# A decoder layer on one core: the first loads in another order and on a second queue, early transposes moved, and the sample-state products grouped in other blocks

## The chip, the core and the metric

One NeuronCore of one Trainium2 chip runs the whole program. The metric is device microseconds (us) of one launch, the median of several runs. Engines: TensorE (PE in the profile; its weight loads are PEld), VectorE (DVE), ScalarE (ACT), GpSimd (POOL) and SyncE (SP, which here only issues DMAs). "q" behind an engine's name means its instruction queue, where DMAs are issued.

## The reference

One inference step of one layer (`DEPTH` is 1) for 256 prompt tokens and 8 x 4 sample tokens, all in fp32, model width 2048:

```python
proj = x @ w_in
gB, gC, h, q, k, v, z, b_logit, a_logit, m_a, m_b = jnp.split(proj, split_points, axis=-1)
conv_out, new_conv_a = causal_depthwise_conv(gC * h, conv_a_buf, conv_a_w)
y_a = (gB * conv_out) @ w_a_out
qkv, new_gdn_buf = causal_depthwise_conv(jnp.concatenate([q, k, v], -1), gdn_buf, gdn_conv_w)
...
o, S = gated_delta_rule(qh, kh, vh, g, beta, S0.astype(jnp.float32))
o = o * lax.rsqrt(jnp.mean(o * o, -1, keepdims=True) + NORM_EPS) * gdn_norm_w
o = o * jax.nn.silu(z)
y_b = o @ w_b_out
merged = jax.nn.sigmoid(m_a) * y_a + jax.nn.sigmoid(m_b) * y_b
x = layer_norm(ALPHA * x + merged @ w_o, ln1_g, ln1_b)
hid = jnp.square(jax.nn.relu(x @ w_up))
x = layer_norm(ALPHA * x + hid @ w_down, ln2_g, ln2_b)
```

It returns the two outputs and the new convolution and delta-rule states. The delta rule keeps a 128 x 128 state S for each of 8 heads of each sample; the new sample states are an output of 4 MB.

## The kernel before, in words

**Tokens as columns.** All 288 tokens (256 prompt, 32 sample) are the moving columns of TensorE's products; 128 x 128 pieces of the weights are the stationary operand. x arrives token by row, so TensorE turns it (transposes against `ident`, L965 for prompt, L949 for samples) into tiles of 128 features by 288 tokens. Every fp32 factor is split into a high and a low part (`xh`, `xl`; `hi`, `lo`), and each product is done as three: `xh*hi` and `xl*hi` (L216), `xh*lo` (L218).

**Blocks.** The weights are cut into blocks of 512 KB (`blocks`), and the main loop (L1672) goes through them one by one. A block passes four steps: `load(i)` brings `raw` by a DMA issued on SyncE's queue (L174); `split_hi` casts it to `hi` on ScalarE (L184); `split_lo` subtracts on VectorE, `lo = raw - hi` (L139), and with that frees the `raw` buffer; `matmuls(i)` does its 24 products. `raw`, `hi` and `lo` have four buffers each. In the steady part, loop step i casts and subtracts for block i + 3 (`AHEAD`) at its beginning and issues the load of block i + 7 at its end. That load has to wait for `split_lo` of block i + 3, which frees the buffer. Every engine works its instructions in the order in which the loop emits them.

**The first block.** Block 0 is two groups of columns for half the depth: for `k` = 0, 1 and for each of the two `members` (`u`), six products: two `xh*hi`, two `xl*hi`, two `xh*lo`. Its raw weights come in parts: `w_first(0, 0, 1)` and `w_first(0, 1, 2)` are the halves for k = 0 (128 KB each), `w_first(1)` the 256 KB for k = 1. x comes in parts as well: `x_first(a, b)` brings columns a to b of the first 512 features. `fill` is a list of closures; `matmuls` pops one behind each `xh*lo` product. `second_tile` (two turns, the copies of x for k = 1, and the casts of the weights for k = 1) and `second_half` (the turns for the next block's two tiles) are put there. `warm_up(n, u)` issues n products of zeros on `128 * u` columns, which nothing reads.

**The sample states.** The generator `gdn(G)` does the delta rule of head group G, and its inner generator `sample` (L1447) the samples' part; both run one step per block, between the casts and the block's products. At its end `sample` goes over four heads `hh`: `spread(hh)` makes `vm[hh]` by eight ScalarE multiplications (L1496); for `j` = 0, 1 a product of 512 columns (`pn`, L1508) goes to one of four PSUM buffers (`gtile`), and four VectorE instructions add it to `S0[:, hh]` (L142, `S<-S,gexp,g`) and with that free the buffer; `store(hh - 1)` sends 512 KB of new states out on GpSimd's queue (L1517). `spread(hh + 1)` is emitted at the beginning of head `hh`. A `yield` before a product moves it to the next block; for G = 1 two of the eight products have none and stand in one block with the product before them.

**Around it, at blocks 106 to 112** (392 to 415 us in the trace): the same blocks carry, in `gdn(1)`, the output norm: squares on ScalarE (L1574, L1575), a scaling (`sq`, L1578), a square root with its table load (L1580), then on VectorE `so`, the reciprocal (L1581), a scaling of the output `xt` (L139) and its transpose (L1585). The loop emits `split_lo` behind them. Block 111 also holds the evacuation of z's third group (`sz`, L384, with a table load for Silu), which stands on ScalarE behind the cast for block 114; it frees the PSUM buffer `acc` into which block 112 (the first of the merge gates) begins to write.

Of the kernel before, what the change touches and what calls it, by code (L numbers as in the profile page):

```python
# [16 lines left out]
P = 128  # L17
# [13 lines left out]
C_GB, C_GC, C_H, C_Q, C_K, C_V, C_Z, C_BA, C_MA, C_MB = (  # L31
    0, 1024, 2048, 3072, 4096, 5120, 6144, 7168, 7184, 9232)

GW = 256
# [67 lines left out]
def hybrid_kernel(ctx: ExitStack, tc: tile.TileContext, A):  # L102
# [16 lines left out]
    def nm(s):  # L119
        counter[0] += 1  # L120
        return f"{s}{counter[0]}"
# [13 lines left out]
    act, dve, pe, gps, sp = nc.scalar, nc.vector, nc.tensor, nc.gpsimd, nc.sync  # L135
# [11 lines left out]
    w_in = A["w_in"][0]  # L147
# [8 lines left out]
    raw, his, los = {}, {}, {}  # L156
    due = {}
    fill = []
# [5 lines left out]
    def load(i, steps=(), between=()):  # L164
        if i >= len(blocks):
            return
        gi, r0, k0, _, _ = blocks[i]
        t = wp.tile([P, KB, GW], F32, tag="raw", name=nm("raw"))
        kb, cols = gi["kb"], gi["cols"]
        dst = t.rearrange("p k c -> p (k c)").rearrange("p (k c) -> p k c", k=kb)  # L170
        src = gi["W"][r0:r0 + kb * P, gi["col0"]:gi["col0"] + cols].rearrange("(k p) c -> p k c", p=P)
        k = 0
        for step in steps or (kb,):
            sp.dma_start(dst[:, k:k + step], src[:, k:k + step])  # L174
            k += step
            if between:
                between.pop(0)()
        raw[i] = t
# [14 lines left out]
    def matmuls(i):  # L193
        gi, r0, k0, first, last = blocks[i]
        if gi.get("by_token"):
            return first_tokens(i, k0)
        members = gi.get("pair", (gi,))
        if first:
            for m in members:
                m["ps"] = acp.tile([P, 2, 512], F32, tag="acc", name=nm("acc"))  # L200
        ps = members[0]["ps"]
        h, l = his.pop(i), los.pop(i)
        ah, al = gi["acts"]()
        n = gi["width"]
        kb = gi["kb"]
        h, l = (u.rearrange("p k c -> p (k c)").rearrange("p (k c) -> p k c", k=kb) for u in (h, l))
        for k in range(kb):
            xh_, xl_ = ah[:, k0 + k, 0:n], al[:, k0 + k, 0:n]
            st = first and k == 0
            en = last and k == kb - 1  # L210
            per = gi["cols"] // P // len(members)
            for u, m in enumerate(members):
                ts = [(m["ps"][:, t, 0:n], slice((per * u + t) * P, (per * u + t + 1) * P)) for t in range(per)]
                both = [(o, c, x) for o, c in ts for x in (xh_, xl_)]
                for o, c, x in both[::2] + both[1::2] if i == 0 else both:
                    pe.matmul(o, h[:, k, c], x, start=st and x is xh_, stop=False)  # L216
                for o, c in ts:
                    pe.matmul(o, l[:, k, c], xh_, start=False, stop=en)  # L218
                    if fill:
                        fill.pop(0)()  # L220
        if last:
            for n, f in enumerate(gi["evac"]):
                at(i + 1 + n, lambda f=f: f(ps))
# [666 lines left out]
    def warm_up(n, u=4):  # L890
        for _ in range(n):
            pe.matmul(wps.rearrange("p (u c) -> p u c", u=4)[:, 0:u], warm, bmid(warm, u), start=True, stop=True)
# [14 lines left out]
    def x_first(a, b):  # L907
        sp.dma_start(xr[0][:, :, a:b], xpr[:, :, a:b])
# [1 line left out]
    def x_sample_in(c, queue=sp):  # L910
        queue.dma_start(xs4[:, c * P:c * P + P], xsr[c])

    def w_first(k, a=0, b=2):
        sp.dma_start(raw[0][:, 2 * k + a:2 * k + b, :],
                     w_in[k * P:k * P + P, C_K + GW * a:C_K + GW * b].rearrange("p (u c) -> p u c", c=GW))

    x_first(0, 128)
    x_sample_in(0, act)
    w_first(0, 0, 1)
    w_first(0, 1, 2)  # L920
    x_first(128, 512)
    w_first(1)
    load(1)
    sp.dma_start(xr[1], xpr[:, :, 512:1024])
    x_sample_in(1)
# [21 lines left out]
    def x_sample(i):  # L947
        g = gtile()
        pe.transpose(g[:, 0:P], xs4[:, i * P:(i + 1) * P], ident)  # L949
        gv = g[:, 0:P].rearrange("p (t j) -> p j t", j=4)  # L950
        xv, xw = (u[:, 4 * i:4 * i + 4, NP_:NT] for u in (xh, xl))

        def out(copy=act.copy):
            copy(xv, gv)  # L954
            tt(xw, gv, xv, SUB)
        return out
# [188 lines left out]
    def gdn(G):  # L1145
# [214 lines left out]
        both = Tm.rearrange("p q (j k) -> p q j k", j=8)  # L1360
# [86 lines left out]
        def sample():  # L1447

            sp1 = gtile()
            pe.matmul(sp1[:, 0:128], kst, kst, start=True, stop=True)  # L1450
            pe.matmul(sp1[:, 128:256], kst, qst, start=True, stop=True)
            pe.transpose(sp1[:, 384:512], vfs.rearrange("p h b t -> p (h b t)"), ident)
            stt(Es, G_["s_row"][:, G], G_["s_ngc"][:, G:G + 1], cst("mbias4"), ADD, ADD)
            act.activation(Es, Es, AF.Exp)
            act.mul(vs, sp1[:, 384:512], snk)
            act.mul(kr, kr, sc[:, 0:1])
            stt(nMs, sp1[:, 0:128], sc[:, 2:3], Es, MUL, MUL)
            stt(aTs, sp1[:, 128:256], srk, Es, MUL, MUL)
            n4, u4, t4, r4 = (Ts[:, 4 * u:4 * u + (16 if u == 3 else 4)] for u in range(4))
            dve.tensor_reduce(out=n4, in_=nMs.rearrange("p (b j) -> p j b", j=4), axis=mybir.AxisListType.X, op=ADD)  # L1460
            tt(n4, n4, cst("i4u"), MUL)
            tt(n4, n4, cst("i4"), ADD)
            sp.dma_start(four_d[G].rearrange("b k j -> (b k) j"), n4)
            yield
            sp.dma_start(r4, four_d[G].rearrange("b k j -> b (k j)").unsqueeze(1).to_broadcast([32, 4, 16]))
            yield from quarters(kr3, kr, 0)
            if G:
                yield
            rows4 = r4.rearrange("p (k j) -> p k j", k=4)
            dve.tensor_copy(u4, cst("i4"))  # L1470
            for j in range(1, 4):
                tt(t4[:, 0:j + 1], u4[:, 0:j + 1], rows4[:, 0:j + 1, j], MUL)
                dve.tensor_reduce(out=u4[:, j:j + 1], in_=t4[:, 0:j + 1], axis=mybir.AxisListType.X, op=ADD)
            tt(Us.rearrange("p (b j) -> p b j", j=4), u4.unsqueeze(1).to_broadcast([P, 32, 4]),
               cst("l4").rearrange("p (b j) -> p b j", j=4), MUL)
            stt(vs, kso[:, 0, :], G_["s_neg"][:, G:G + 1], vs, MUL, ADD)
            act.mul(osm, kso[:, 1, :], G_["s_eg"][:, G:G + 1])
            yield
            pv_ = gtile()
            pe.matmul(pv_[:, 0:P], Us, vs, start=True, stop=True)  # L1480
            act.mul(vns, pv_[:, 0:P], sc[:, 1:2])
            v3 = pl.tile([P, 4, P], F32R, tag="U", name=nm("v3"))
            yield from quarters(v3, vns, 1)
            yield
            po = gtile()
            pe.matmul(po[:, 0:P], aTs, vns, start=True, stop=True)
            tt(osm, osm, po[:, 0:P], ADD)
            done.append(1)
            vm = {}


            def spread(hh):
                if hh < 4:
                    vm[hh] = pl.tile([P, 8, P], F32R, tag=("vmh", "vml")[hh % 2], name=nm("vm"))
                    for b in range(8):
                        act.mul(vm[hh][:, b], v3[:, hh].bitcast(F32), cst("bmask")[:, b:b + 1])  # L1496

            spread(0)
            yield
            for hh in range(4):  # L1500
                spread(hh + 1)
                if hh:
                    store(hh - 1)
                for j in range(2):
                    if G == 0 or (hh, j) not in ((2, 0), (3, 1)):
                        yield
                    pn = gtile()
                    pe.matmul(pn, kr3[:, hh], vm[hh][:, 4 * j:4 * j + 4, :], start=True, stop=True)  # L1508
                    for u in range(4):
                        b = 4 * j + u  # L1510
                        stt(S0[:, hh, b], S0[:, hh, b], G_["egls"][:, b, 4 * G + hh:4 * G + hh + 1],
                            pn[:, u * P:u * P + P], MUL, ADD)
            yield
            store(3)
# [9 lines left out]
        o = T([P, 4, 2, P], "xt")  # L1524
# [123 lines left out]
    idle = lambda: None  # L1648
    turns(t0[0:2])
    xs_out = x_sample(0)  # L1650
    warm_up(1, 2)
    act.copy(h0[:, 0], t[:, 0])
    o0[0](dve.tensor_copy)
# [1 line left out]
    tt(l0[:, 0], t[:, 0], h0[:, 0], SUB)  # L1655
    act.copy(h0[:, 1], t[:, 1])
    tt(l0[:, 1], t[:, 1], h0[:, 1], SUB)
    fill.extend([second_tile, idle, idle, idle, second_half])
    rest = [lambda: sp.dma_start(cf[:, 128:], A["cf"][:, 128:NE]),
            lambda: sp.dma_start(cfe, A["cf"][:, NE:NL]),  # L1660
            lambda: sp.dma_start(wbar, w_in[:, C_BA:C_BA + 16].rearrange("(k p) c -> p k c", p=P)),
# [137 lines left out]
```

## Time and profile before

| | us |
|---|---|
| median of 3 runs (lowest, highest) | 1654.21 (1653.01, 1655.17) |
| the profiled execution's own time | 1654.0 |
| its span, first to last instruction | 1652.2 |
| TensorE busy | 1644.3 |
| VectorE busy | 986.2 |
| ScalarE busy | 781.6 |
| GpSimd busy | 139.3 |
| moved by DMA | 282.49 MB |

A row of the timeline gives the start and length of a run of equal instructions in us, the engine, the line, the operation, the tile written and those read, and in square brackets how long the engine had been idle before it and what ended that. Matmuls are pipelined: a row's length contains the time through the array, so the pace is read from start to start. The granted clock of TensorE, a column of the view by stretches, is 0.999 over the run.

### The profile page before, as it was taken

What the parts mean: (1) busy time and instruction counts of PE and PEld (TensorE: products, weight loads), DVE (VectorE), ACT (ScalarE), POOL (GpSimd) and SP (SyncE); (2) the same over time, 40 slices, a digit from 0 to 9 for tenths busy, and PEclk for the clock granted to TensorE, in tenths of its full rate; (3) what the DMA queues carried; (4) which work ended last, traced back from release to release, by engine and by line L of the source; (5) the groups of instructions that cost most, each with busy time, mean ns of one, the idle gap of its engine ahead of it and who ended that gap; (6) DMA issues with size and microseconds to landing.
All of it is one profiled execution on the core that took longest, in us unless ns stands there. A gap on an engine that the chain in (4) does not pass through costs nothing.

```text
span 1652.2 us, 30937 instructions
## 1 busy us (share of the span) xinstructions
PE 1644.3 (100%) x12856; PEld 1630.8 (99%) x12856; DVE 986.2 (60%) x1340; ACT 781.6 (47%) x1222; POOL 139.3 (8%) x286
## 2 busy tenths in 40 slices
PE   9999999999999999999999999999999999999998
PEld 8999999999999999999999999999999999999998
DVE  6787688867544444457776666444444444444466
ACT  6774678357533333334454454443334433344354
POOL 1132214234000000000000000000000000000111
PEclk9999999999999999999999999999999999999999
DMA  8567466746655555555565555555555555555653
GB/s 254 174 183 210 140 174 198 213 129 169 200 165 165 166 165 165 166 165 162 172 215 157 172 163 166 165 165 166 166 165 165 166 166 166 166 166 166 180 163 100
DMA packets 278855, 282.49 MB, mean 171 GB/s; under 512 B 15059, under 2 KB 272648, under 8 KB 278452
## 3 DMA queue, kind: packets, MB, share of 16 engines
q1 hardware_dynamic: 274538, 268.81, 54.3%
q0 software_dynamic: 4032, 11.63, 2.4%
q8 instruction: 101, 1.65, 0.4%
q14 instruction: 40, 0.33, 0.1%
q10 hardware_dynamic: 144, 0.07, 0.0%
HBM read 272.83 MB, written 7.63 MB: 170 GB/s over the span
## 4 chain that ended last, share of the span: by engine, by line
PE 98%; ACT 1%; DMA 1%; DVE 1%; issue 0%; SPq 0%; ACTq 0%
PE acc L216 63%; PE acc L218 31%; PE acc L747 1%; PE g L1530 0%; PE g L1550 0%; PE g L1553 0%; DMA raw<-in_w_in_dram 0%; DMA xr<-in_x_prompt_dram 0%; PE g L1336 0%; PE g L1236 0%; ACT hi L184 0%; PE g L1542 0%; ACT b L1574 0%; PE g L1345 0%; PE g L965 0%; DVE Y L142 0%
## 5 line engine op out<-in xcount | busy, mean ns | idle before, releaser
L139 DVE TENSOR_TENSOR lo<-raw,hi 128x1024 fp32r<-128x1024 f32 (+1 forms) x503 | 607.1, 1211 | 557.7 <-ACT hi L184 556.7
L184 ACT CAST hi<-raw 128x1024 fp32r<-128x1024 f32 (+1 forms) x499 | 518.6, 1042 | 721.0 <-PE acc L216 633.5
L216 PE MATMUL acc<-xh,hi 128*128 128x288 f32 x1408 | 398.1, 298 | 0.4 <-ACT xh L954 0.2
L216 PE MATMUL acc<-xl,hi 128*128 128x288 f32 x1408 | 394.7, 296 | 0.0
L218 PE MATMUL acc<-xh,lo 128*128 128x288 f32 x1408 | 303.3, 296 | 0.0
L216 PE MATMUL acc<-dl,hi 128*128 128x288 f32 (+1 forms) x1024 | 287.7, 295 | 0.0
L216 PE MATMUL acc<-dh,hi 128*128 128x288 f32 (+1 forms) x1024 | 287.4, 295 | 0.0
L216 PE MATMUL acc<-hl,hi 128*128 128x288 f32 x992 | 277.8, 295 | 0.0
L216 PE MATMUL acc<-hh,hi 128*128 128x288 f32 x992 | 277.4, 294 | 0.0
L216 PEld LDWEIGHTS acc<-xh,hi 128*128 128x128 f32 x1408 | 265.1, 189 | 3.2 <-issue 1.3
L216 PEld LDWEIGHTS acc<-xl,hi 128*128 128x128 f32 x1408 | 264.9, 188 | 0.7
L218 PEld LDWEIGHTS acc<-xh,lo 128*128 128x128 f32 x1408 | 226.7, 188 | 0.2 <-DVE lo L139 0.2
L218 PE MATMUL acc<-dh,lo 128*128 128x288 f32 (+1 forms) x1024 | 219.8, 296 | 0.0
L218 PE MATMUL acc<-hh,lo 128*128 128x288 f32 x992 | 213.2, 296 | 0.0
L216 PEld LDWEIGHTS acc<-dh,hi 128*128 128x128 f32 x1024 | 193.3, 189 | 0.0
L216 PEld LDWEIGHTS acc<-dl,hi 128*128 128x128 f32 x1024 | 192.8, 188 | 0.0
L216 PEld LDWEIGHTS acc<-hh,hi 128*128 128x128 f32 x992 | 186.3, 188 | 0.4 <-issue 0.4
L216 PEld LDWEIGHTS acc<-hl,hi 128*128 128x128 f32 x992 | 186.1, 188 | 0.0
L218 PEld LDWEIGHTS acc<-dh,lo 128*128 128x128 f32 x1024 | 164.6, 188 | 0.0
L218 PEld LDWEIGHTS acc<-hh,lo 128*128 128x128 f32 x992 | 159.1, 188 | 0.0
L216 PE MATMUL acc<-mh,hi 128*128 128x288 f32 x256 | 71.9, 297 | 0.0
L216 PE MATMUL acc<-ml,hi 128*128 128x288 f32 x256 | 71.7, 295 | 0.0
(421 smaller groups left out, 1478.9 us busy)
## 6 DMA issues: line engine op xcount, KB each, us to landing
raw<-in_w_in_dram SPq DMA_DIRECT2D x175, 512.0 KB, 3.8
raw<-in_w_up_dram SPq DMA_DIRECT2D x128, 512.0 KB, 3.8
raw<-in_w_down_dram SPq DMA_DIRECT2D x128, 512.0 KB, 3.5
raw<-in_w_o_dram SPq DMA_DIRECT2D x32, 512.0 KB, 3.6
raw<-in_w_a_out_dram SPq DMA_DIRECT2D x16, 512.0 KB, 4.3
raw<-in_w_b_out_dram SPq DMA_DIRECT2D x16, 512.0 KB, 3.6
out_dram<-S POOLq DMA_DIRECT2D x8, 512.0 KB, 4.6
S<-in_state_gdn_dram POOLq DMA_DIRECT2D x4, 512.0 KB, 6.3
```

Of the source, the lines that this page charges most:

```text
L139: dve.tensor_tensor(out=out, in0=a, in1=b, op=op)
L184: act.copy(his[i][:, k:k + step], raw[i][:, k:k + step])
L216: pe.matmul(o, h[:, k, c], x, start=st and x is xh_, stop=False)
L218: pe.matmul(o, l[:, k, c], xh_, start=False, stop=en)
L747: pe.matmul(out, x[:, kk, c], w[:, k, :], start=False, stop=stop)
```

## The change

```diff
@@ matmuls
-                for o, c, x in both[::2] + both[1::2] if i == 0 else both:
+                for n_, (o, c, x) in enumerate(both[::2] + both[1::2] if i == 0 else both):
                     pe.matmul(o, h[:, k, c], x, start=st and x is xh_, stop=False)
+                    if i == 0 and k == 0 and u == 1 and n_ == 1:
+                        fill.pop(0)()
@@ first loads
-    def w_first(k, a=0, b=2):
-        sp.dma_start(raw[0][:, 2 * k + a:2 * k + b, :],
+    def w_first(k, a=0, b=2, queue=sp):
+        queue.dma_start(raw[0][:, 2 * k + a:2 * k + b, :],
...
     x_first(0, 128)
     x_sample_in(0, act)
     w_first(0, 0, 1)
-    w_first(0, 1, 2)
-    x_first(128, 512)
+    w_first(0, 1, 2, act)
+    x_first(128, 256)
     w_first(1)
+    x_first(256, 512)
     load(1)
@@ sample, in gdn
-                    if G == 0 or (hh, j) not in ((2, 0), (3, 1)):
+                    if G == 0 or (hh, j) not in ((1, 1), (2, 1)):
                         yield
@@ before the loop
     xs_out = x_sample(0)
+    warm_up(1)
     warm_up(1, 2)
...
-    fill.extend([second_tile, idle, idle, idle, second_half])
+    fill.extend([idle, idle, second_tile, idle, idle, second_half])
```

The second half of block 0's first weights is issued on ScalarE's queue, behind the samples' x. The part of x of 384 columns becomes two of 128 and 256, with the weights for k = 1 between them. One warm-up product of 512 columns is added before the one of 256. `second_tile` moves from behind the fifth product of block 0 to behind the eighth (six of u = 0, two of u = 1); `second_half` stays behind the fifth product of k = 1. For G = 1 the products (hh, j) stand in blocks as: before (0,0) | (0,1) | (1,0) | (1,1) (2,0) | (2,1) | (3,0) (3,1); after (0,0) | (0,1) | (1,0) (1,1) | (2,0) (2,1) | (3,0) | (3,1). With them, `spread(3)` and `store(1)` are emitted one block earlier, in block 106, right behind the squares of the output norm. All other instructions keep their order.

More of the change, by code (lines that the diff above doesn't have):

```diff
@@ L911, in x_sample_in @@
         queue.dma_start(xs4[:, c * P:c * P + P], xsr[c])
-    def w_first(k, a=0, b=2):
-        sp.dma_start(raw[0][:, 2 * k + a:2 * k + b, :],
-                     w_in[k * P:k * P + P, C_K + GW * a:C_K + GW * b].rearrange("p (u c) -> p u c", c=GW))
+    def w_first(k, a=0, b=2, queue=sp):
+        queue.dma_start(raw[0][:, 2 * k + a:2 * k + b, :],
+                        w_in[k * P:k * P + P, C_K + GW * a:C_K + GW * b].rearrange("p (u c) -> p u c", c=GW))
     x_first(0, 128)
```

## The prediction, made before the changed kernel ran

> **What bounds the kernel now.** First the page: the engines' busy time and the chain that ended last, then its table of DMA issues.
>
> ```profile
> span 1652.2 us, 30937 instructions
> PE 98%; ACT 1%; DMA 1%; DVE 1%; issue 0%; SPq 0%; ACTq 0%
> raw<-in_w_in_dram SPq DMA_DIRECT2D x175, 512.0 KB, 3.8
> out_dram<-S POOLq DMA_DIRECT2D x8, 512.0 KB, 4.6
> ```
>
> TensorE holds 98% of the chain. So only what keeps it from its next product counts, and two places are touched: the first 12 us and blocks 106 to 112. The views of who waited for whom, TensorE's and that of its weight loads, give one wait each in the second place.
>
> ```profile
> PE g L1508 <- DVE S L142: 0.5, 1, 0.5
> PEld acc L216 <- ACT sz L384: 0.4, 1, 0.4
> ```
>
> The timeline of the first 12 us:
>
> ```profile
> 0.74 0.62 ACTq L911 DMA_DIRECT2D xs<-in_x_sample_dram  x1
> 0.99 2.31 PE L892 MATMUL g<-warm 128*128 128x512 bf16 x5 [0.99 <-DVE warm L887]
> 1.25 0.93 SPq L914 DMA_DIRECT2D raw<-in_w_in_dram  x2
> 1.39 1.28 ACT L1652 ACT_TABLE_LOAD   x1 [1.39 <-PEq L1786]
> 3.17 0.66 PE L965 MATMUL g<-cf,xr 128*128 128x128 f32 x2
> 3.80 0.40 ACT L1652 CAST hi<-raw 128x256 fp32r<-128x256 f32 x1 [1.13 <-DMA raw<-in_w_in_dram]
> 3.84 0.42 PE L892 MATMUL g<-warm 128*128 128x256 bf16 x1
> 4.44 0.83 PE L216 MATMUL acc<-xh,hi 128*128 128x288 f32 x2 [0.18 <-ACT xh L954]
> 4.54 0.40 ACT L1656 CAST hi<-raw 128x256 fp32r<-128x256 f32 x1 [0.17 <-DMA raw<-in_w_in_dram]
> 5.65 0.44 PE L218 MATMUL acc<-xh,lo 128*128 128x288 f32 x1
> 6.52 0.69 PE L965 MATMUL g<-cf,xr 128*128 128x128 f32 x2 [0.43 <-DMA xr<-in_x_prompt_dram]
> 7.25 0.68 PE L216 MATMUL acc<-xh,hi 128*128 128x288 f32 x2
> 7.25 0.37 ACT L971 CAST xh<-g 128x256 fp32r<-128x256 f32 x1 [2.31 <-PE g L965]
> 7.52 0.71 ACT L1630 CAST hi<-raw 128x256 fp32r<-128x256 f32 x2
> 8.69 0.68 PE L216 MATMUL acc<-xh,hi 128*128 128x288 f32 x2
> 9.89 0.61 PE L965 MATMUL g<-cf,xr 128*128 128x128 f32 x4
> 10.85 1.15 ACT L184 CAST hi<-raw 128x512 fp32r<-128x512 f32 x2
> 11.54 0.40 PE L216 MATMUL acc<-xh,hi 128*128 128x288 f32 x1
> ```
>
> Two things are to be seen. The turn at 6.52 waits for x's 384 columns, with five products done and seven that could run. And the pace is slow: from 7.25 to 8.69 six products start, 0.24 us each. By stretches:
>
> ```profile
> 6.90:10.00 3.10, 3.10 (x15) 3.08 (x14) 1.09 (x3) 0.98 (x3) 0.00 (x0) 1.00 0.99 353
> 11.50:20.00 8.50, 8.46 (x64) 8.30 (x65) 6.81 (x12) 5.07 (x10) 0.00 (x0) 1.00 1.04 338
> ```
>
> From 11.5 on, 64 start in 8.5 us, 0.13 each. The clock column reads 1.00 in both, so it doesn't show this change of pace. The four turns at 9.89 take 0.61 us, about what two took at 6.52 (0.69), so the pace changes at about 9.9, which is 3.4 us after the wait at 6.52.
>
> The timeline around block 107:
>
> ```profile
> 393.45 1.11 DVE L142 SCALAR_TENSOR_TENSOR S<-S,gexp,g 128x128 f32<-128x128 f32 x4
> 397.38 0.19 ACT L1575 ACTIVATION_READ_ACCUMULATOR b<-osm 128x1 f32 x1
> 397.47 1.03 ACT L184 CAST hi<-raw 128x1024 fp32r<-128x1024 f32 x1
> 398.65 0.17 DVE L142 SCALAR_TENSOR_TENSOR so<-so,sq 128x9 f32<-128x9 f32 x1 [2.94 <-ACT sq L1578]
> 400.82 2.44 ACT L1496 ACTIVATE vm<-v,cf 128x128 fp32r<-128x128 f32 x8
> 402.94 2.11 DVE L142 SCALAR_TENSOR_TENSOR S<-S,gexp,g 128x128 f32<-128x128 f32 x8
> 403.29 0.39 PE L1508 MATMUL g<-vm,kr 128*128 128x512 f32 x1
> 404.17 0.47 PE L1508 MATMUL g<-vm,kr 128*128 128x512 f32 x1 [0.49 <-DVE S L142]
> 404.32 0.93 POOL L1517 DMA_DIRECT2D out_dram<-S  x1 [5.24 <-DVE S L142]
> 404.98 1.22 DVE L139 TENSOR_TENSOR lo<-raw,hi 128x1024 fp32r<-128x1024 f32 x1
> 406.26 2.53 SPq L174 DMA_DIRECT2D raw<-in_w_in_dram  x2
> 408.31 0.43 PE L218 MATMUL acc<-xh,lo 128*128 128x288 f32 x2
> 411.39 1.05 ACT L184 CAST hi<-raw 128x1024 fp32r<-128x1024 f32 x1 [1.66 <-DMA raw<-in_w_in_dram]
> 412.46 1.28 ACT L384 ACT_TABLE_LOAD   x1
> 413.75 0.65 ACT L384 ACTIVATE sz<-acc 128x576 f32<-128x576 f32 x1
> 413.89 0.43 PE L218 MATMUL acc<-xh,lo 128*128 128x288 f32 x2
> 414.46 0.40 PE L216 MATMUL acc<-xh,hi 128*128 128x288 f32 x1
> ```
>
> VectorE idles 2.94 us for ScalarE's `sq`; everything behind, the eight `S` updates and then the `lo` of block 110, hangs on that. The end of that `lo` (406.20) frees a raw buffer, and the load for block 114 goes out at 406.26. Its cast at 411.39 waited for this DMA, 5.1 us from issue. Behind the cast stand the table load and `sz`, which ends at 414.40; block 112 starts at 414.46, 0.3 us later than the pace allows (413.89 plus two products).
>
> **The start, part by part.** The second weight half leaves SyncE's queue: the two issues there take 0.93, so x's next part goes out 0.47 earlier and is a third as large. On ScalarE the half is issued behind 0.74 + 0.62 and moves the table load from 1.39 to about 1.85, an estimate with the same 0.47. It then ends near 3.1, still covered by the wait for weights until 3.80. If the half came later than by SyncE, its cast (4.54) has cover until the seventh product, near 6.1; a delay of more than 1.5 us would show.
>
> The extra warm-up product starts at 3.84 and takes 0.46 (2.31 / 5); the old one, half as wide, takes 0.23 behind it, so TensorE is free at 4.53 rather than at 4.44: 0.1 us lost at most, in a gap that was idle anyway.
>
> `second_tile` then stands behind eight products instead of five. At 0.24 us the sixth starts near 5.9, where TensorE idled, the turns near 6.6 with their data there (they came at 6.5 as the tail of 384 columns, and are now 128 of them). ScalarE's copy came 0.73 after the turns (7.25 against 6.52) and its first cast ends 0.63 behind that (7.52 + 0.36); so k = 1 starts at about 8.05 instead of 8.69: 0.6 us gained. If the slow pace still lasts until 9.9, that is all.
>
> What decides is the pace. If it is set by 3.4 us without a break, as here from 6.5 to 9.9, then without the break it changes 3.4 us after 4.5, at 7.9. Then k = 1 needs 5 x 0.13 to its turns (8.7), and the next block follows these after 1.65 (11.54 against 9.89), at 10.35: 1.2 us gained, which I take. The bounds: 0.6 lower if the weights' half comes late by more than its cover (a gain of 0.0), and 2.2 if the pace is fast from the first product, when the turns come near 7.7 and block 1 at 9.35.
>
> The Trainium skill, in "TensorE: Matmul & The Clock Gate" (Part 4, PE-mode transpose), speaks against this: transposes don't count as busy in the way products do. By it the turns now amid block 0 might break the busy time, and the gain would be the 0.6 of the slow pace. The rows do not bear that out: the stretch from 6.52 to 9.9 begins with two turns.
>
> **The sample products.** The pair at 403.29 and 404.17 is split, so the wait of 0.49 goes; the new pairs find their buffers free, because the updates of (1, 0) at 393.45 and of (1, 1), now right behind them, end by 395.7. In exchange `spread(3)`, 2.44 us on ScalarE, moves from 400.82 to right behind the squares (their last row is 397.38), ahead of the cast at 397.47 and of `sq`. What is late next:
> 1. `sq` and all that hangs on it, 2.44: the eight `S` updates from 402.94 to 405.4, `lo` of block 110 from 404.98 to 407.4, with its end at 408.65.
> 2. TensorE needs this `lo` at 408.31, less the 0.49 saved, at 407.8: a new wait of 0.8. The casts themselves have two blocks of cover.
> 3. The raw buffer comes free 2.44 later: load of block 114 at 408.7. Landing by the page's median of 3.8: 412.5; by the 5.1 of this very load: 413.8. Cast, table load and `sz` take 3.0 (411.39 to 414.40): `sz` ends at 415.5 to 416.8. Block 112 waits for it, whatever TensorE saved before.
>
> So block 112 starts 1.1 to 2.4 later than 414.46. I take 2.1, near the load's own 5.1, because the neighbour that slowed it is there again: a 512 KB store of states, which `S` updates released at 404.32, ahead of the load at 406.26; now the end of the eight updates (405.4 and 2.1 us) releases one at 407.5, ahead of the load at 408.7.
>
> **Sum.** Start -1.2, pairs +2.1: +0.9. The profiled execution took 1654.0 (1652.2 span and 1.8 around it): 1654.9. The median of the runs stands 0.2 above it: 1655.1 us.
>
> **The rivals.**
> *A, the pairs pay.* If the load lands so early that `sz` is not late, or ScalarE reaches `sq` in time, the 0.49 and the 0.3 before block 112 are won: -0.8, with the start -2.0: 1652.2. For it: the 5.1 is far above the median 3.8. Against: 2.94 us of idle VectorE say that `sq` has no slack, and even 3.8 gives +1.1.
> *B, fast from the start.* With the pace full before 6.6, start -2.2, pairs +2.1: 1654.1. For it: the products of zeros run from 0.99 almost without a gap once the new one is in. Against: before, the turns at 3.17 and the product at 3.84 followed them up to the gap of 0.18 at 4.44, and nothing came of it. Together with A it is 1651.2. The Trainium skill ("TensorE: Matmul & The Clock Gate", Part 1) has the pace follow a free-running window of about 3.4 us. By that rule the moment would differ between runs between 0 and 3.4 us behind the earliest.
> *C, slower: the load stands behind the store.* Released at 407.5, the store takes the page's 4.6 to land, 412.1; if the load moves only then, its 3.8 ends at 415.9 instead of 413.8. `sz` ends at 418.9, pairs +4.4: 1657.4. From a landing at 412.6 on the pairs cost more than the start's 1.2 gives; 0.2% slower takes a landing at 415.9, or at 414.7 where the start gives nothing. For it: this load took 1.3 more than the median beside the same store. Against: the two shared the engines then, and it was 5.1, not 8.
> *D, the start doesn't do what it says.* If block 1's own weights land no earlier than its casts at 10.85, nothing is gained there: 1656.3. Against: these casts follow ScalarE's copies with no DMA wait.
>
> **The numbers.** Forecast 0.45, A 0.20, B 0.13, C 0.12, D 0.10. The likeliest's own range is 1653.8 to 1656.0 (pairs 1.1 to 2.4, start 0.6 to 1.5). With A's 1652.2 and C's 1657.4 just outside: 1652.3 to 1657.2. About 0.2% (3.3 us) is what a measurement of this kernel can tell from no change; faster than that needs A with B and some more: 0.06; slower needs C with a start that gives less than 1.2, or both terms beyond their bounds: 0.12; the rest, 0.82, lies within.
>
> **What would show it.** Right: no TensorE wait for x near 6.5; products at 0.13 us before 9; block 1 near 10.4; `sq` 2.4 us later behind the squares than before; a TensorE wait for `lo` in block 110; block 112 released by `sz` again, more than 1 us late. Wrong: block 112 without a wait for `sz` (then A), a pace that changes at 9.9 or later, or a cast for block 114 that doesn't wait for its DMA.

## The result, and the profile after

| | before | after |
|---|---|---|
| median (lowest, highest; runs) | 1653.97 (1652.60, 1655.17; 14) | 1657.60 (1655.66, 1660.19; 14) |
| ratio, 95% interval | | 1.0022 [1.0015, 1.0029] |
| profiled execution's own time, span | 1654.0, 1652.2 | 1656.6, 1654.9 |

The change costs 3.6 us where the sum had 0.9. The profiled execution is one of the quicker ones of its kernel and carries 2.6 of the 3.6. The first two lines are from its page (span, and chain of waits by engine), the others from the view of what TensorE waited for (total, number of waits, longest).

```profile
span 1654.9 us, 30941 instructions
PE 96%; DVE 1%; ACT 1%; DMA 0%; issue 0%; POOL 0%; ACTq 0%; DVEq 0%; SPq 0%
```

```profile
PE acc L216 <- ACT sz L386: 2.1, 1, 2.1
PE acc L216 <- ACT hi L184: 0.9, 1, 0.9
PE acc L220 <- DVE lo L139: 0.8, 1, 0.8
PE acc L216 <- DVE xl L139: 0.4, 1, 0.4
```

The waits of 0.5 for `S` and of 0.4 for x are gone. Three are new: for `hi` in block 1, for `xl` in block 6 and for `lo` in block 110. The one for `sz` ahead of block 112 has grown from 0.4, where only the weight loads showed it, to 2.1. The timeline, start first:

```profile
3.82 0.84 PE L894 MATMUL g<-warm 128*128 128x512 bf16 x2
4.59 0.85 PE L216 MATMUL acc<-xh,hi 128*128 128x288 f32 x2
5.24 0.52 PE L216 MATMUL acc<-xl,hi 128*128 128x288 f32 x2
6.13 0.38 PE L968 MATMUL g<-cf,xr 128*128 128x128 f32 x2
7.28 0.53 PE L216 MATMUL acc<-xh,hi 128*128 128x288 f32 x2 [0.24 <-ACT hi L1633]
9.81 1.14 ACT L184 CAST hi<-raw 128x512 fp32r<-128x512 f32 x2 [0.69 <-DMA raw<-in_w_in_dram]
10.48 0.40 PE L216 MATMUL acc<-xh,hi 128*128 128x288 f32 x1 [0.89 <-ACT hi L184]
17.18 1.05 ACT L184 CAST hi<-raw 128x1024 fp32r<-128x1024 f32 x1 [0.88 <-DMA raw<-in_w_in_dram]
18.26 1.22 DVE L139 TENSOR_TENSOR lo<-raw,hi 128x1024 fp32r<-128x1024 f32 x1 [0.70 <-ACT hi L184]
19.41 1.24 DVE L991 STREAM_TRANSPOSE xtb<-xr 128x1024 f32<-128x1024 f32 x1
20.71 5.20 POOL L998 COPY xm<-xtb 32x256 f32<-32x256 f32 x10 [19.29 <-DVE xtb L991]
25.94 1.14 ACT L1003 CAST xh<-xm 128x512 fp32r<-128x512 f32 x2 [1.00 <-POOL xm L998]
29.21 0.28 DVE L139 TENSOR_TENSOR xl<-g,xh 128x128 fp32r<-128x128 f32 x1
29.55 0.40 PE L216 MATMUL acc<-xl,hi 128*128 128x288 f32 x1 [0.45 <-DVE xl L139]
```

The turns at 6.13 wait for nothing, and the pace is full from about 5.4 on (a pair of products comes to have length 0.52 rather than 0.85; the trace's record of the granted clock begins at 5.44, and in the kernel before at 9.90, so ahead of that the column of the clock tells nothing). Block 1 starts at 10.48 instead of 11.54. Then the lead runs into x's last quarter: block 4's weights land late (17.18), the turn of that quarter stands behind their subtraction on VectorE (19.41), GpSimd's moves take 5.2, and block 6 waits. The same two rows before show how little room there was:

```profile
29.63 0.28 DVE L139 TENSOR_TENSOR xl<-g,xh 128x128 fp32r<-128x128 f32 x1
30.00 0.38 PE L216 MATMUL acc<-xl,hi 128*128 128x288 f32 x1
```

There `xl` ended 0.09 ahead of its product. Now blocks 106 to 112 of the changed kernel:

```profile
397.25 0.19 ACT L1578 ACTIVATION_READ_ACCUMULATOR b<-osm 128x1 f32 x1
397.35 2.44 ACT L1499 ACTIVATE vm<-v,cf 128x128 fp32r<-128x128 f32 x8
400.62 0.21 ACT L1581 ACTIVATE sq<-ss 128x9 f32<-128x9 f32 x1
400.86 0.17 DVE L142 SCALAR_TENSOR_TENSOR so<-so,sq 128x9 f32<-128x9 f32 x1 [4.26 <-ACT sq L1581]
405.16 2.12 DVE L142 SCALAR_TENSOR_TENSOR S<-S,gexp,g 128x128 f32<-128x128 f32 x8
407.19 1.22 DVE L139 TENSOR_TENSOR lo<-raw,hi 128x1024 fp32r<-128x1024 f32 x1
407.56 0.89 POOL L1520 DMA_DIRECT2D out_dram<-S  x1 [7.49 <-DVE S L142]
408.46 0.53 PE L220 MATMUL acc<-xh,lo 128*128 128x288 f32 x2 [0.85 <-DVE lo L139]
408.47 2.50 SPq L174 DMA_DIRECT2D raw<-in_w_in_dram  x2
413.61 1.05 ACT L184 CAST hi<-raw 128x1024 fp32r<-128x1024 f32 x1 [2.71 <-DMA raw<-in_w_in_dram]
415.97 0.65 ACT L386 ACTIVATE sz<-acc 128x576 f32<-128x576 f32 x1
416.67 0.40 PE L216 MATMUL acc<-xh,hi 128*128 128x288 f32 x1 [2.11 <-ACT sz L386]
```

This is the predicted order, row for row: `spread(3)` behind the squares, `sq` late, then the eight updates, `lo` of block 110, the load of block 114 (its cast starts 5.1 us after issue, again), and `sz`. The starts of equal products, from the two traces:

| product | before | after | shift |
|---|---|---|---|
| first of block 1 | 11.54 | 10.48 | -1.06 |
| block 6, shown above | 30.00 | 29.55 | -0.45 |
| first of block 106 | 393.03 | 393.14 | +0.11 |
| first of block 109 | 404.48 | 403.62 | -0.86 |
| first of block 112 | 414.46 | 416.67 | +2.21 |

So in this execution the start is worth nothing at block 106, and the pairs cost 2.1. (Behind block 6 another 0.3 of the lead went at block 89, in a wait for `U`, and 0.2 at block 106, which now holds two sample products ahead of this one.) The last product is late by 2.22 (1646.02 against 1643.80), and the span by 2.64: 0.4 lies behind it, in the last outputs. One more number stands in the list of runs: the mean granted clock of each. Of the 14 runs, nine show 0.998 (mean 1658.16) and five 0.999 (mean 1656.37; the profiled run is one of these). The runs at 0.998 lose on average 1.8 us that this trace does not show.

### The profile page after: what moved, and what is told of

It is laid out like the page before. It is cut to its first block, busy times and chain, and to the rows that moved or that the text cites. A ratio compares the mean times of both kernels' runs of the same rounds, so it can differ in the third digit from the quotient of the medians.

```text
span 1654.9 us, 30941 instructions
## 1 busy us (share of the span) xinstructions
PE 1643.0 (99%) x12857; PEld 1629.4 (98%) x12857; DVE 986.2 (60%) x1340; ACT 782.0 (47%) x1222; POOL 137.5 (8%) x286
## 3 DMA queue, kind: packets, MB, share of 16 engines
q0 software_dynamic: 4032, 11.63, 2.5%
## 4 chain that ended last, share of the span: by engine, by line
PE 96%; DVE 1%; ACT 1%; DMA 0%; issue 0%; POOL 0%; ACTq 0%; DVEq 0%; SPq 0%
PE acc L216 61%; PE acc L220 31%; PE acc L749 1%; PE g L1533 0%; PE g L1553 0%; PE g L1556 0%; DVE lo L139 0%; DMA raw<-in_w_in_dram 0%; PE g L1339 0%; ACT hi L184 0%; PE g L1239 0%; PE g L1545 0%; ACT b L1577 0%; PE g L1348 0%; DVE Y L142 0%
```

## The experiments

All in one table; "0.998" counts the runs whose mean granted clock is 0.998 or less. The kernel before, run beside e1 to e12, shows it in 5 of 89 runs. The figure is a sign and not a proof: in the traces the clock also falls to half 2.0 to 4.9 us before the span ends, which moves the mean too, and the three runs of e7 and e9 at 0.998 are no slower than their others.

| run | median (lowest, highest; runs) | ratio to before, 95% | 0.998 |
|---|---|---|---|
| the change | 1657.60 (1655.66, 1660.19; 14) | 1.0022 [1.0015, 1.0029] | 9 |
| e1 pairs alone | 1656.50 (1655.26, 1659.50; 11) | 1.0016 [1.0007, 1.0024] | 5 |
| e2 start alone | 1654.13 (1653.31, 1655.36; 11) | 1.0001 [0.9992, 1.0010] | 0 |
| e4 start, SyncE only | 1654.44 (1653.92, 1656.07; 11) | 1.0004 [0.9995, 1.0013] | 1 |
| e3 pairs behind `sq` | 1653.06 (1651.65, 1654.92; 11) | 0.9995 [0.9986, 1.0004] | 2 |
| e8 same pairs, `spread(3)` late | 1655.51 (1653.91, 1658.80; 11) | 1.0008 [0.9999, 1.0017] | 5 |
| e12 `lo` first | 1653.49 (1653.04, 1654.11; 11) | 0.9997 [0.9988, 1.0006] | 0 |
| e5 change, break filled | 1656.68 (1655.49, 1657.17; 11) | 1.0016 [1.0007, 1.0025] | 0 |
| e6 break of 2.2 | 1656.18 (1654.57, 1658.66; 11) | 1.0012 [1.0004, 1.0021] | 4 |
| e10 break of 4.4 | 1659.34 (1658.36, 1660.86; 5) | 1.0034 [1.0021, 1.0046] | 5 |
| e11 break of 4.4, filled | 1657.85 (1656.88, 1660.01; 7) | 1.0026 [1.0015, 1.0037] | 0 |
| e7 start and e3 | 1652.86 (1652.42, 1654.36; 11) | 0.9994 [0.9986, 1.0003] | 1 |
| e9 e7 and x earlier | 1652.39 (1651.63, 1653.67; 11) | 0.9991 [0.9983, 1.0000] | 2 |

### The two halves alone

e1, the pairs alone:

```diff
-                    if G == 0 or (hh, j) not in ((2, 0), (3, 1)):
+                    if G == 0 or (hh, j) not in ((1, 1), (2, 1)):
```

> The kernel before with only the sample products regrouped. Theory 1 (the whole loss is the order on ScalarE: spread(3) ahead of sq, so lo of block 110, load of block 114, sz and block 112 are late; the start nets nothing): +2.2 in the profile at block 112, with a wait of TensorE for sz of about 2 us, and a median of 1656.1 to 1657.6. Theory 2 (the start itself costs about 1 in the typical run): as theory 1 in the profile, but a median about 1 below that of the full change, 1656.3 or less. Theory 3 (the load of block 114 stands behind the store more often than in the one profile): median at or above 1657.6, a landing of that load later than 413.6.

Most of the loss is the pairs': 2.5 of 3.6 in the median, with the wait for `sz` of 2.1 in the trace. The span of its profiled run, 1657.7, is 5.5 above that of the kernel before: 1.8 were lost at the start (block 1 at 13.35 rather than 11.54), 2.2 at blocks 106 to 112, and 1.5 were in no theory. The view by stretches of e1 (from and to, length, busy time with instructions of TensorE, weight loads, VectorE, ScalarE and GpSimd, then TensorE's granted clock, the DMA share and GB/s), from the break ahead of block 112 on:

```profile
416.15:418.42 2.27, 0.14 (x2) 0.00 (x1) 1.23 (x1) 2.24 (x4) 1.23 (x2) 1.00 0.92 269
418.42:419.38 0.96, 0.96 (x6) 0.96 (x7) 0.86 (x2) 0.88 (x1) 0.00 (x0) 0.92 0.87 287
419.38:422.70 3.32, 3.32 (x15) 3.32 (x15) 1.91 (x2) 0.76 (x2) 0.00 (x0) 0.51 1.04 350
422.70:426.02 3.32, 3.32 (x27) 3.32 (x26) 2.24 (x2) 3.06 (x3) 0.00 (x0) 1.00 0.47 156
```

About 1 us behind the break the granted clock falls to half: 15 products in 3.32 us, 0.24 apart, where 25 fit at 0.133. (The trace's record of the clock has 0.5 for 3.41 us, from 419.23 to 422.65; the row begins with the first slow product.) After the wait is over, e1's lag behind the kernel before thus grows from 3.96 us at block 112's first product to 5.51 at the last product of all, 1.5 us more. Such a stretch lowers the mean over 1655 us by 0.001: the three traces that hold one (e1, e8, e10) have means of 0.9980 to 0.9981, the eleven others 0.9985 to 0.9994. That fits the change's nine runs at 0.998. In the change's own profiled run the break is as long and nothing follows:

```profile
414.40:416.67 2.27, 0.16 (x2) 0.00 (x1) 1.22 (x1) 2.24 (x4) 1.24 (x2) 1.00 0.99 283
417.63:420.95 3.32, 3.32 (x27) 3.32 (x26) 1.91 (x2) 0.88 (x2) 0.00 (x0) 1.00 1.04 345
```

e2, the start alone (the line above undone in the changed kernel), and e4, e2 with ScalarE's queue undone:

```diff
-    w_first(0, 1, 2, act)
+    w_first(0, 1, 2)
```

> The change with the sample products grouped as before, so the start alone. Theory 1 (the 1.8 us won in block 0 is given back to block 1's own weights and to x's last quarter): between -0.4 and 0 at block 106 and at the end, 1653.6 to 1654.0, no wait for sz above 0.5. Theory 2 (the start itself costs): 1654.7 to 1655.2. The prediction's step: -1.2, 1652.8.

> The start alone as in e2, but the second half of the first weights stays on SyncE's queue. If ScalarE's queue causes the one DMA engine that is about 1.1 us late from 6 to 7 us on: no such straggler here, block 1 at 10.0 or earlier rather than 10.5, 0.3 to 0.5 faster than e2 there. If the straggler is chance: e2 and e4 differ by less than 0.3 at block 1 and in the median. In either case the part of x for the first turns comes 0.47 later than in e2.

The start is worth nothing in the median (+0.1 and +0.4, both inside the interval), near theory 1's numbers; neither -1.2 nor a loss of 1. The traces fit theory 1 only in part: in e4's the lead was gone in block 6, in e2's 0.86 of it was left at block 106 and 0.78 at block 112. With SyncE alone block 4's weights were late as well (cast at 17.68 in e4, 16.63 in e2, 17.18 in the change), so ScalarE's queue is not what makes them late; e4's block 1 started at 10.66, later than e2's 10.37.

### Is it the order on ScalarE?

e12, the full change, with only `lo` of block 110 emitted ahead of the norm and the updates:

```diff
+        if i == mark["merge"] - 5:
+            split_lo(i + ahead)
         if i > 7 and sgen:
...
-        if i > 5 and not late:
+        if i > 5 and not late and i != mark["merge"] - 5:
             split_lo(i + ahead)
```

> The full change, with the subtraction for block 110 emitted ahead of the norm's scaling and the eight updates in that one block, and nothing else. Theory 1 (the loss runs from the late sq through the updates and lo of block 110 to the load of block 114 and sz): lo of block 110 begins by 401, the load of block 114 goes out near 402, no wait for lo in block 110 and none for sz in block 112; 1653.2 to 1654.0, so 3.6 or more below the full change. Rival (the store or the pairs' other work delays sz anyway): a wait of 1 or more stays at block 112, 1655 or above.

Its timeline (two rows), and then its view of TensorE's waits:

```profile
399.73 0.21 ACT L1581 ACTIVATE sq<-ss 128x9 f32<-128x9 f32 x1
399.86 1.23 DVE L139 TENSOR_TENSOR lo<-raw,hi 128x1024 fp32r<-128x1024 f32 x1 [4.15 <-ACT hi L184]
```

```profile
PE acc L216 <- ACT sz L386: 0.4, 1, 0.4
```

`sq` is as late behind the squares as in the change, and yet the loss is gone: 4.1 us in the median, by moving one instruction of VectorE. The wait for `sz` is back to the 0.4 shown here. So late `sq` costs only through the `lo` that is queued behind it and the load which that `lo` frees.

e3 groups the products otherwise and puts `spread(3)` and `store(1)` behind `sq`; e8 does the same with exactly the change's grouping:

```diff
             for hh in range(4):
+                if G and hh == 2:
+                    yield
                 spread(hh + 1)
...
-                    if G == 0 or (hh, j) not in ((2, 0), (3, 1)):
+                    if G == 0 or (hh, j) not in ((1, 1), (2, 0), (3, 1)):   # e3
+                    if G == 0 or (hh, j) not in ((1, 1), (2, 0), (2, 1)):   # e8
```

> The start as before; the products (hh, j) as (0,0) | (0,1) | (1,0) (1,1) | (2,0) | (2,1) | (3,0) (3,1), and spread(3) and store(1) emitted one block later, behind sq. Theory 1 (the order on ScalarE is what costs): the wait of 0.49 is gone, sq no later than before, the eight updates become four in that block so lo of block 110 ends about 1 us earlier than before, the load of block 114 goes out near 405.2, no wait for sz: -0.5 to -0.8, 1653.2 to 1653.5. Rival (the regrouping itself costs, by the two products in one block): a wait in block 106 or 109 in its place, 1654 or more.

> The start as before, the products grouped exactly as in the change, (1,0) (1,1) and (2,0) (2,1) together, but spread(3) and store(1) emitted one block later, behind sq. Theory 1 (the place of spread(3) ahead of sq is the whole loss of the pairs): sq no later than before, the eight updates where they were, lo of block 110 near 405, load of block 114 near 406.3, sz wait 0 to 0.5 in the profile, and no loss: 1653.7 to 1654.0. Rival (the grouping itself makes the eight updates or a product late): a loss of 1 or more stays, 1655 or above.

e3's trace came out as expected, with no TensorE wait for `S`, `lo` or `sz`; its -0.95 is a little past the range, and its interval still includes no change. e8 did not: 1655.5 rather than 1654. Its timeline and its view by stretches:

```profile
400.55 2.43 ACT L1496 ACTIVATE vm<-v,cf 128x128 fp32r<-128x128 f32 x8
401.91 0.58 PE L1510 MATMUL g<-vm,kr 128*128 128x512 f32 x1 [1.91 <-issue]
```

```profile
402.29:405.61 3.32, 3.32 (x15) 3.31 (x14) 3.32 (x10) 3.14 (x8) 0.53 (x1) 0.51 0.16 58
```

The change's grouping puts (3, 0) into block 108, which starts near 400; the product waits until four of `spread(3)`'s eight instructions are done (400.55 and four times 0.30), which the expectation had overlooked. So with this grouping one of two things is late, `sq` or `vm`; and here too a break of about 2 us (400.0 to 401.91) is followed by a stretch at half clock, in another place and without `sz`.

### What a break costs

e5, the full change, with products that nothing reads in the break:

```diff
+        if i == mark["merge"]:
+            g = gtile()
+            for _ in range(15):
+                pe.matmul(g[:, 0:n], h[:, 0, 0:P], ah[:, k0, 0:n], start=True, stop=True)
         for k in range(kb):
```

> The full change with 15 products of 288 columns, which nothing reads, put on TensorE ahead of block 112's first product; at 0.133 us each they take 2.0 of the 2.27 us for which TensorE stands idle there. Theory P (a break this long makes TensorE's pace fall to half for some 3.3 us in many runs, as in the profile of the pairs alone, which costs about 1.5 each time): no half pace in block 112, the wait for sz still ends when it did, and the median is 0.7 to 1.2 below the full change's 1657.6, so 1656.4 to 1656.9, with a narrower spread. Rival (the part of the loss beyond the 2.2 lies elsewhere: the loads, the start or the tail): no change, 1657.3 to 1657.9.

0.9 below the change, the spread 1.7 us instead of 4.5, and none of 11 runs at 0.998 instead of nine of 14. The two intervals against the kernel before overlap; it is the count that separates them, and the change's five runs at 0.999 (mean 1656.4) are as fast as e5's (1656.6). Work that delivers nothing made the typical run faster. e6 and e10 leave the change out and make the break in the kernel before, by 3 and by 6 copies; e11 is e10 with 29 products in the break, as in e5:

```diff
         def f(ps):
             sz = gd["pool"].tile([P, 2, NT], F32, tag="hs", name=nm("sz"))
+            for _ in range(3 if p == 2 else 0):    # e10, e11: 6
+                act.copy(sz, ps[:, :, 0:NT])
             act.activation(sz, ps[:, :, 0:NT], AF.Silu)
```

> The kernel before with three copies (0.65 us each) put on ScalarE ahead of sz, nothing else: sz ends 1.95 later and TensorE's wait at block 112 becomes about 2.2, as long as in the full change. Theory P (half pace after such a break, in part of the runs): +1.95 and 0.7 to 1.2 more in the median, 1656.7 to 1657.2, and a wide spread of the runs (4 us or more). Rival (the wait costs its own length): +1.95, 1655.9 to 1656.1, and before's spread.

> The kernel before with six copies ahead of sz instead of e6's three: the wait at block 112 becomes about 4.1 to 4.2. Theory P (half pace for some 3.3 us after a long enough break, at 0.11 us lost per product): now in nearly every run, so +3.9 and 1.0 to 1.6 more, 1658.8 to 1659.5, with products 0.24 apart in block 112 or 113 in the profile. Rival (a wait costs its own length): +3.9, 1657.8 to 1658.1.

> e10 with 29 products that nothing reads (0.133 us each, 3.9 in all) on TensorE in that wait. Theory P: no half pace, +3.9 and no more, 1657.7 to 1658.1, 1.0 to 1.6 below e10. Rival: the same time as e10.

e10 and e11 came out as theory P had them: with the break filled, 1.5 us less in the median, for a break of the same length. (The two traces differ by 3.1 in span; 1.6 of that is the start, block 1 at 11.63 in e10 and 10.01 in e11, and 1.5 is the half clock.) The views by stretches, of e10 (break, and half clock) and then of e11 (the break filled, and what follows):

```profile
414.50:418.91 4.41, 0.06 (x1) 0.00 (x0) 0.00 (x0) 4.29 (x7) 0.91 (x2) 1.00 1.00 313
419.74:423.06 3.32, 3.32 (x15) 3.32 (x15) 2.00 (x4) 1.91 (x4) 0.00 (x0) 0.51 0.34 83
```

```profile
412.90:417.34 4.44, 3.97 (x32) 3.74 (x30) 0.00 (x0) 4.32 (x7) 1.00 (x2) 1.00 0.99 321
417.34:420.66 3.32, 3.32 (x25) 3.32 (x26) 2.77 (x3) 1.91 (x3) 0.00 (x0) 1.00 0.38 137
```

e6 missed its number by 0.5, and its median lies 0.1 above the rival's range, so the median alone does not decide. Its spread was as wide as expected (4.1), but only 4 of 11 runs show the lower clock (mean 1657.5, the other seven 1655.4), so the median fell among the others. By this sign a break of 2.0 to 2.3 us sets off the half clock in part of the runs (4, 5 and 9 of 11, 11 and 14 in e6, e1 and the change), one of 4.4 in all five.

The traces show what decides. In all fourteen the record of the granted clock changes only at whole steps of 3.413 us, counted from its first full clock near the start: in e1, which begins at 13.05, after 119 and 120 steps, in e8 after 115 and 116, in e10 after 120 and 121, and in every trace after 480 to 482 steps behind the last product. On this grid, the steps that hold a break, with TensorE's busy time from the view by stretches:

| run | step, from and to | TensorE busy | clock in the next step |
|---|---|---|---|
| the change | 411.63 to 415.04 | 2.93 | 1.00 |
| e6 | 410.52 to 413.93 | 2.50 | 1.00 |
| e6 | 413.93 to 417.34 | 2.32 | 1.00 |
| e10 | 412.76 to 416.17 | 1.80 | 1.00 |
| the change | 415.04 to 418.45 | 1.78 | 1.00 |
| e8 | 398.72 to 402.13 | 1.50 | 0.50 |
| e1 | 415.82 to 419.23 | 1.28 | 0.50 |
| e10 | 416.17 to 419.58 | 0.67 | 0.50 |

So a break costs extra when enough of it falls into one step: the change's break was split between two, e1's, as long, lay in one. An estimate from these rows: the limit lies between 1.63 and 1.91 us of idle time in a step, and a break of 2.27 us that falls anywhere on the grid passes it in 0.55 to 0.71 of the cases (9 of 14 runs in the change and 5 of 11 in e1 show 0.998); one of 4.41 always does. No run moved a break along the grid, and the limit holds for full products: at the end of e7, where turns and small products stand, a step with 2.30 us busy was followed by half clock too.

### Where the start's lead goes

e7 is the change's start with e3's pairs. e9 is e7 with x's last quarter loaded and turned ahead of block 4's weights:

```diff
+    sp.dma_start(xr[3], xpr[:, :, 1536:2048])
     load(4)
...
+        if i == 2:
+            x_turn()
+            x_moves(gps.tensor_copy, range(10))
         if i < 6:
             for u, step in {0: ((1, 2),), 1: ((2, 1), (3, KB))}.get(i, ((i + 2, KB),)):
                 split_hi(u, step)
                 split_lo(u, step)
-        if i == 2:
-            x_turn()
-            x_moves(gps.tensor_copy, range(10))
```

> The start of the change with the grouping of e3 (spread(3) behind sq). If the start of the change is worth nothing in the median: as e3, 1653.0 to 1653.3. If it is worth the 0.5 to 0.8 that it showed in the profile of e2: 1652.3 to 1652.6. If it costs 0.1 to 0.4, as the medians of e2 and e4 would have it: 1653.2 to 1653.5.

> e7 with x's last quarter loaded ahead of block 4's weights, and its turn on VectorE and its moves on GpSimd emitted ahead of block 4's cast and subtraction. Theory G (what is won at the start is taken back in block 6, where x's last quarter comes late because its turn stands behind the weights of block 4): that turn begins 0.7 to 1.5 earlier than in e7 (19.90), TensorE's wait of 0.8 for it in block 6 is gone, the lead at block 1 of about 1.2 over the kernel before is still there at block 106, and the median is 0.5 to 1.0 below e7's 1652.9: 1651.9 to 1652.4. Rival (block 4's weights, now later, take the lead in its place): a wait for hi or lo in block 4, the same time as e7.

e7 stands 0.2 below e3: again the start brings next to nothing, and its trace has a wait of 0.8 for `xl` in block 6, where a lead of 1.2 at block 1 has turned into a lag of 0.07. e9's timeline:

```profile
17.45 1.24 DVE L990 STREAM_TRANSPOSE xtb<-xr 128x1024 f32<-128x1024 f32 x1
19.08 1.05 ACT L184 CAST hi<-raw 128x1024 fp32r<-128x1024 f32 x1 [2.80 <-DMA raw<-in_w_in_dram]
28.26 0.28 DVE L139 TENSOR_TENSOR xl<-g,xh 128x128 fp32r<-128x128 f32 x1
28.96 0.29 PE L216 MATMUL acc<-xl,hi 128*128 128x288 f32 x1
```

The turn begins at 17.45 (19.90 in e7), block 4's weights come later (19.08) without harm, and the product follows `xl` without a wait. The lead of 1.10 in block 1 is there until block 88, and 0.65 of it at block 106. The median is 0.5 below e7's, which is as theory G had it but less than these runs can separate. e9 is the fastest version of all: 1.5 below the kernel before, at the bound of its interval, and 5.2 below the change.

## Why the prediction was wrong

*Forecast 1655.1, measured 1657.6.* Two steps of the sum failed, by a little over 1 each.

*"Start -1.2".* Right: no wait for x, and products 0.13 apart well before 9. That block 1 came at 10.48, where 10.35 was forecast, is luck: the pace was full at 5.4 and not at 7.9, which would have put block 1 at 9.59, and its own weights, whose wait the forecast put at nothing, then held it for 0.89. The failed step is the gain itself and its way to the end. It was measured against one trace, whose slow first 10 us the old start does not always have: block 1 begins between 10.01 and 13.35 in the seven traces with the old start, between 9.59 and 10.66 in the seven with the new one. And the lead was followed only as far as block 1; the next thing that could come late was not looked for: `xl` in block 6, which had 0.09 us of room in the profile of before and stops TensorE for 0.4 to 0.8 in five of the six traces with the new start and the old order of x's last quarter. The medians of e2 (+0.1) and of e7 against e3 (-0.2) can't be told from nothing; e9, which takes the wait for `xl` away, still has 0.65 of the lead at block 106 of its trace. Rival D named the right kind of cause, and its wait came as well; it missed the place behind it. The lower bound given for the start does not add up: 1.2 less 0.6 is 0.6, not 0.0, and the range went by 0.6.

*"Pairs +2.1".* Right in every row for the wait itself: `sq` late, `lo` in block 110 with 0.85 (0.8 forecast), the load's 5.1, and block 112 at +2.2; e12 shows that this chain is the cause. What the sum lacks is a term for what follows a break of TensorE. The wait was costed at its length; nine of 14 runs show the lower mean clock of a stretch at half clock, and are 1.8 us slower on average, so 9/14 of 1.8 is 1.15. The five runs at 0.999 stand 2.4 above before's mean of 1653.93, near the 2.1. e5, e10 and e11 show the term by itself.

*The rivals.* A was wrong: `sz` had no slack. C was wrong: the load took 5.1 beside the store, not 8. B's condition came true, a pace that is full before 6.6, but not its time: the 2.2 it gave the start were not there. The pace at the start is not fixed by the program. Taking the first of its own products that start less than 0.15 us apart, the old start had its full pace at 10.5, 13.1, 5.3, 5.5, 10.3, 10.6 and 6.8 us in the seven profiles that hold it, the new one between 5.0 and 7.2 in seven. I took one profile's 9.9 for a property of the kernel.

*The rule that was weighed.* The turns amid block 0 did not keep the pace down: it was full at 5.4, before the turns at 6.13 began, and stayed so through them. So the gain was not held to the 0.6 of the slow pace, but these rows do not test the rule of the Trainium skill quoted in the prediction, since the pace was full ahead of the turns.

*What stays open.* The lower clock goes with 1.8 us in the change (1.9 in e1, 2.8 in e8), one stretch in a trace with 1.5; what the rest is was not traced, since the list of runs has no timeline. The two halves alone add up to 2.6 of the 3.6, within the intervals. The Trainium skill gives a free-running window of about 3.4 us ("TensorE: Matmul & The Clock Gate", Part 1); the steps of 3.413 us on which the clock changes in these traces agree with it. That it is the place of a break on this grid that differs from run to run rests on five traces.

## What to carry to other kernels

Follow a gain beyond the wait that it removes to the next operand whose producer is only just in time: here the 0.09 us of room in block 6 deserved as much attention as the first block. When an instruction moves on an in-order engine, ask which transfer the work queued behind it frees; moving one subtraction by one place (e12) repaired what moving one ScalarE step had cost. And don't price a break of TensorE at its length alone: read the granted clock behind it, in more than one execution, and remove the break, or fill it with products that nothing reads.

## What was not expected of the hardware

After a break of 2.27 us (e1; 1.91 in e8) TensorE's granted clock was 0.50 for 3.41 us, beginning 0.2 to 0.8 us after the break, and by the list of runs in part of the runs of one and the same program. The Trainium skill ("TensorE: Matmul & The Clock Gate", "Why this matters for your kernels") sets the bound for such gaps at about 3 us; here 2.27 and 1.91 were enough where they fell into one step of the grid, and the measurement decides. A difference of 0.001 in the mean granted clock of a run hints at such a stretch in the list of runs.
